# Delta-net layer: pair scales on VectorE, later transposes of keys and first values, head convolutions in two parts, gate sums beside the decays

## The chip, the core and the metric

The kernel runs on one core of a Trainium2 chip. The metric is the device time of one execution in microseconds. A core has five engines that run side by side and wait for each other by semaphores: TensorE (PE, matmuls; its weight loads, PEld, overlap them), VectorE (DVE), ScalarE (ACT), GpSimd (POOL), and SyncE (SP), which here issues most of the DMAs. Matmuls write to PSUM, of which this kernel keeps two pools of four banks, `ps` (tiles named `mm`) and `ps_acc` (tiles named `acc`); everything else lives in SBUF.

## What is computed

A trunk of two layers over 256 tokens of width 1024. Each layer is a SwiGLU block, a mixer and another SwiGLU block, with RMS norms around each. The mixer of the first layer is a short gated convolution, that of the second a gated delta-net with 8 key heads and 16 value heads of width 128. The change lies in the delta-net alone. Its core, cut down:

```python
qkv = silu(causal_depthwise_conv(x @ w_qkv, conv_w))         # width 4
q, k = l2norm(q), l2norm(k)                                   # repeated for two value heads each
beta = sigmoid(b); g = -exp(a_log) * softplus(a + dt_bias)    # per token and value head
g = cumsum(g) in a chunk
decay = exp(g_c - g_s) below the diagonal
a = strict_lower(beta * (k @ k.T) * decay)
t_inv = inverse(eye + a)
u, w = t_inv @ (beta * v), t_inv @ (beta * k * exp(g))
for each chunk:
    v_new = u - w @ state
    o = (q * exp(g)) @ state + lower(q @ k.T * decay) @ v_new
    state = state * exp(g_last) + (k * exp(g_last - g)).T @ v_new
return (o * rsqrt(mean(o * o) + eps) * norm_w * silu(z)) @ w_out
```

## The kernel before

The tokens are two tiles of 128 (`NT`), and a chunk here is one such tile. Every weight matrix streams from HBM in units of 128 x 1024 floats. `unit` (L108) loads one into `raw`, ScalarE rounds it to `whi` (L117), and VectorE takes the rest, `wlo = raw - whi` (L119); three matmuls then stand for one of full precision. Three `raw` buffers and eight of each half bound how far the stream runs ahead.

The layer's stream on TensorE is: the head (`head_slabs`, L218 to L222) with the gates' columns and the first seven key and query tiles, for both token tiles; nine key and query tiles in groups of 24 matmuls of 256 columns (`stat_group`, L275 to L277); three slabs of z (`act_group`, L218 to L222, 512 columns); four slabs of values (`v_group`, four `stat_group`s each); the last slab of z; the output projection (`out_proj`, L320 to L322).

Beside this stream run chains, Python generators under a `Ticker` (L89). A tick falls after every 12 matmuls of `stat_group` (two in a group) and after every 6 of `act_group` (eight in a slab of z, both token tiles together). `yield k` puts the rest of a chain k ticks further back in the text of the program. The text sets a priority only: the build works out when the operands of each instruction should be ready, orders every engine's queue by that and by the text, and what it puts out is fixed. An engine works through its queue in order, so an instruction whose operands come later than the build expected holds up all that follow. `tc.issue_after` adds an order by hand.

The chains that matter here:

- `gates` (L504) works out beta and the log decays g on POOL, ACT and DVE, and ends with two small matmuls (L531, L532) that sum g along a tile, and their exponentials `etail` and `eg`.
- `decays` (L536) multiplies a triangle with g (`gu`, mostly L545 on DVE), waits until a convolved head is there (`convs`), and then makes the eight decay tiles: a matmul (L553), an exponential (L555), a mask on POOL (L556). Two pairs' tiles are written in one tick, the others in the next; a tick later the silus of the waiting heads follow.
- `head_tail` (L888) transposes the head's last tile and convolves the seven head tiles. `conv` (L580) is one ACT operation (L581) and three DVE operations (L583). `kq_raw` calls it for a key or query tile and, when a head has both, passes the head on to silu (L570).
- `kq_chain` (L602) takes the heads in four pairs. Each head, `KQ_WAIT` ticks after its silu, is transposed (L615) and multiplied with itself (L618); ACT squares and sums the transposed tiles (L627). A tick after the second head, the sums get EPS (L631, POOL), keys are inverted (L633, DVE), `dd` = beta / |k|^2 (L636, POOL), and eight DVE operations (L642) write the scaled and decayed products, which frees their PSUM. ACT copies the diagonal blocks of 32 to `Ld` (L649). POOL also makes `nk` (a power, L651), `eq` and `wt`. After the last pair `invert` starts.
- `invert` (L664) inverts all 32 blocks' diagonals at once: a transpose (L666), 31 steps of two DVE operations (L674, L676), two transposes (L678, L680). `INV_WAIT` ticks later TensorE joins the blocks in two halves (L704 to L736), with the diagonals copied into `E` (L696) and `KQ` (L686) by POOL.
- `v_pair` (L745) convolves two value tiles, takes their silu, waits `V_WAIT` ticks, transposes them (L754) and scales them into `nv`. Its buffer `vc` is named `yb`, of which there are two.
- `scan` (L794) of a pair starts when its values and its inverse are there: solves (L768), products inside a chunk (L777), the state (L808, L817), and the same for the second tile; `z_chain` (L838) applies the norm and z, transposes (L848) and splits the result into the operands of the output projection (L851, L852).

Of the kernel before, what the change touches and what calls it, by code (L numbers as in the profile page):

```python
# [10 lines left out]
ALU = mybir.AluOpType  # L11
# [4 lines left out]
NT = 2  # L16
D = 1024
KD = D // P
# [3 lines left out]
NG = 4  # L22
B32 = 32
EPS = 1e-6
# [5 lines left out]
NSMALL = 22  # L30
NBIG = 8
NROW = 3
KQ_WAIT = 3
INV_WAIT = 37
V_WAIT = 4
SCAN_WAIT = 2
ORD = "00111222"
GORD = "00012222"
# [11 lines left out]
def trunk_kernel(ctx: ExitStack, tc: tile.TileContext, x, norm_g, w_gu, w_dn, sc_in, sc_cw, sc_out,  # L50
                 gdn_h0, gdn_h1, gdn_a0, gdn_a1, gdn_a2, gdn_v, gdn_z, gdn_cw, gdn_al, gdn_dt, gdn_nw, gdn_out, eye, upper, slower, out, stop=None):
    nc = tc.nc
    V, S, G, PE = nc.vector, nc.scalar, nc.gpsimd, nc.tensor
# [71 lines left out]
    def slab(shape, dtype, name):  # L125
        return hp.tile(shape, dtype, name=name, tag="slab")

    def big(shape, dtype, name):
        return bp.tile(shape, dtype, name=name, tag="big")
# [343 lines left out]
    def gdn_proj(xh, xl, mid):  # L473
# [22 lines left out]
        def bc(ap, n):  # L496
            return ap.unsqueeze(1).broadcast_to([P, n, ap.shape[-1]])

        def side_bank():
            return (ps if tail[0] else ps_acc).tile([P, 4, P], F32, name="mm" if tail[0] else "acc")  # L500
# [3 lines left out]
        def gates():  # L504
            def sm(name):
                return sp.tile([P, NT, NVH], F32, name=name, bufs=1)

            a, u, e, z, q = sm("ga"), sm("gb"), sm("gc"), sm("gd"), sm("ge")
            G.tensor_tensor(a, ba[:, :, NVH:], bc(dtb, NT), ALU.add)
            G.tensor_scalar(u, a, 0.0, -2.0, ALU.max, ALU.mult)  # L510
            G.tensor_tensor(e, a, u, ALU.add)
            first = S.activation(e, e, AF.Exp).ins
            with tc.issue_after(first):
                S.activation(al, al, AF.Exp)
            S.activation(beta, ba[:, :, 0:NVH], AF.Exp, scale=-1.0)

            V.tensor_scalar(z, e, 2.0, None, ALU.add)
            V.reciprocal(z, z)
            V.tensor_tensor(z, z, e, ALU.mult)
            V.tensor_tensor(u, z, z, ALU.mult)  # L520
            V.tensor_scalar(q, u, 1.0 / 19.0, None, ALU.mult)
            for k in (17, 15, 13, 11, 9, 7, 5, 3):
                V.scalar_tensor_tensor(q, q, 1.0 / k, u, ALU.add, ALU.mult)
            V.scalar_tensor_tensor(q, q, 1.0, z, ALU.add, ALU.mult)
            V.tensor_scalar(a, a, 0.0, None, ALU.max)
            V.scalar_tensor_tensor(q, q, 2.0, a, ALU.mult, ALU.add)
            V.scalar_tensor_tensor(g, q, -1.0, bc(al, NT), ALU.mult, ALU.mult)
            G.tensor_scalar(beta, beta, 1.0, None, ALU.add)
            V.reciprocal(beta, beta)
            pg = side_bank().rearrange("p a b -> p (a b)")[:, 0:2 * NVH].rearrange("p (t n) -> p t n", t=NT)  # L530
            PE.matmul(pg[:, 0, :], lhsT=tri_s, rhs=g[:, 0, :], start=True, stop=True)  # L531
            PE.matmul(pg[:, 1, :], lhsT=tri_u, rhs=g[:, 1, :], start=True, stop=True)  # L532
            S.activation(etail, pg[:, 0, :], AF.Exp)
            S.activation(eg, pg[:, 1, :], AF.Exp)

        def decays():  # L536
            gus = []
            for gi in range(NG):
                gu = big([P, NT, 4, P], F32, "gu")
                for t in range(NT):  # L540
                    if 2 * gi + t < GUACT:
                        for hv in range(4):
                            S.activation(gu[:, t, hv, :], tri_u, AF.Copy, scale=g[:, t, 4 * gi + hv:4 * gi + hv + 1])
                        continue
                    V.tensor_tensor(gu[:, t], bc(tri_u, 4),  # L545
                                    g[:, t, 4 * gi:4 * gi + 4].unsqueeze(2).broadcast_to([P, 4, P]), ALU.mult)
                gus.append(gu)
            while not convs:
                yield 1
            for gi in range(NG):  # L550
                for t in range(NT):
                    pd = side_bank()
                    PE.matmul(pd, lhsT=tri_s, rhs=gus[gi][:, t], start=True, stop=True)  # L553
                    d = slab([P, 4, P], F32, "dec")
                    last_exp[0] = S.activation(d, pd, AF.Exp).ins  # L555
                    G.affine_select(d, d, pattern=[[0, 4], [1, P]], compare_op=ALU.is_ge, fill=0.0, base=0,  # L556
                                    channel_multiplier=-1)
                    dec[t][gi] = d
                if gi % 2:
                    yield 1  # L560
            dec_done[0] = True
            while convs:
                kq_silu(*convs.pop(0))
# [12 lines left out]
        KQ = [[None] * NT for _ in range(NG)]  # L576
# [6 lines left out]
                V.scalar_tensor_tensor(dst[:, j:], src[:, 0:T - j], cw[:, ch, 3 - j:4 - j],  # L583
                                       dst[:, j:], ALU.mult, ALU.add)

        raws, kq_time = {}, [0] * KD

        def kq_raw(kh, c, src):
            if kh not in raws:
                raws[kh] = slab([P, 2, T], F32, "kq")  # L590
            conv(raws[kh][:, c, :], src, c * KD + kh)
            if c == 1:
                if dec_done[0]:
                    kq_silu(kh, raws[kh])
                else:
                    convs.append((kh, raws[kh]))

        def kq_silu(kh, t_):
            silu(t_, t_)
            kq[kh], kq_time[kh] = t_, tk.now  # L600

        def kq_chain():  # L602

            for gi in range(NG):
                ss = sp.tile([P, NT, 2, 2], F32, name="kss", bufs=2)
                k1 = slab([P, 2, 2, P], F32, "kq1")
                pkq = []
                for i in range(2):
                    kh = 2 * gi + i
                    while kq[kh] is None or tk.now < kq_time[kh] + KQ_WAIT:  # L610
                        yield 1
# [16 lines left out]
                    yield 1  # L628
                while dec[1][gi] is None:
                    yield 1  # L630
                G.tensor_scalar(ss, ss, EPS, None, ALU.add)  # L631
                rk = sp.tile([P, NT, 2], F32, name="rk", bufs=2)
                V.reciprocal(rk, ss[:, :, 0, :])  # L633
                dd = small(f"dsc{gi}", 8).rearrange("p (t n) -> p t n", t=NT)
                for t in range(NT):
                    G.tensor_tensor(dd[:, t, :].rearrange("p (k v) -> p k v", k=2),  # L636
                                    beta[:, t, 4 * gi:4 * gi + 4].rearrange("p (k v) -> p k v", k=2),
                                    rk[:, t, :].unsqueeze(2).broadcast_to([P, 2, 2]), ALU.mult)
                for t in range(NT):
# [5 lines left out]
                    for b in range(4):  # L645
                        r = slice(b * B32, (b + 1) * B32)
# [7 lines left out]
                w = small(f"wt{gi}", 4)  # L654
                G.tensor_tensor(w, etail[:, 4 * gi:4 * gi + 4], dd[:, 0, :], ALU.mult)
                Dsc[gi], nk[gi], eq[gi], wt[gi] = dd, n, q, w
                yield 1
            tk.start(invert())


# [3 lines left out]
        def invert():  # L664
# [14 lines left out]
            Yd = row("blk").rearrange("p (a b) -> p a b", a=B32)  # L679
            V.transpose(Yd.rearrange("p h i -> p i h"), X)  # L680
            T1 = row("blk").rearrange("p (a b) -> p a b", a=B32)
            for gi in range(NG):
                for t in range(NT):
                    for b in range(4):
                        r = slice(b * B32, (b + 1) * B32)
                        G.tensor_copy(KQ[gi][t][r, :, 0, r], Yd[r, 8 * gi + t:8 * gi + t + 7:2, :])  # L686
            yield INV_WAIT
            for half in range(2):
                hs = slice(16 * half, 16 * half + 16)
                gis = (2 * half, 2 * half + 1)  # L690
                E = {}
                for gi in gis:
                    E[gi] = slab([P, 8, 64], F32, "E64")
                    for b in range(2):
                        r = slice(b * B32, (b + 1) * B32)
                        G.tensor_copy(E[gi][r, :, r], Xd[r, 8 * gi:8 * gi + 8, :])  # L696
                    G.memset(E[gi][0:B32, :, B32:], 0.0)
                pt = side_bank().rearrange("p a (b c) -> p (a b) c", c=B32)
                for x in range(16):
                    ht = 16 * half + x  # L700
# [5 lines left out]
                for b in (1, 3):  # L706
                    r = slice(b * B32, (b + 1) * B32)
# [37 lines left out]
        def v_pair(gi, i, pt, tiles):  # L745
            vc = sp.tile([P, 2, T], F32, name="yb")
            for j in range(2):
                conv(vc[:, j, :], pt[:, j, :], 16 + 4 * gi + 2 * i + j)
            silu(vc, vc)
            yield V_WAIT  # L750
            tp = ps.tile([P, NT, 2, P], F32, name="mm")
            for t in range(NT):
                for j in range(2):
                    PE.transpose(tp[:, t, j, :], vc[:, j, t * P:(t + 1) * P], ident)  # L754
            for t in range(NT):
                S.activation(tiles[t][:, 2 * i:2 * i + 2, :], tp[:, t, :, :], AF.Copy,
                             scale=nk[gi][:, t, i:i + 1])
            if i == 1:
                nv[gi] = tiles
# [106 lines left out]
        order = [(kh, c) for kh in range(KD) for c in range(2)]  # L866
# [21 lines left out]
        def head_tail(late):  # L888
            yield 1
            late()  # L890
            for kh, c in order[0:7]:
                kq_raw(kh, c, craw[kh][:, c, :])

        tk.start(head_tail(head_slabs([load_slab(gdn_h0, GSPLIT, GORD), load_slab(gdn_h1, GSPLIT, GORD[4:])], xh, xl, evac_head, mid, 0)))
# [148 lines left out]
```

## Time and profile before

| | |
|---|---|
| median of 3 runs | 1130.77 us (1130.25 to 1133.5) |
| the profiled execution | 1131.77 us, of which the span of the profile is 1129.9 us |
| mean granted clock of TensorE | 0.994 of full speed |
| delta-net layer in the profile | head from 664 us, key tiles from 690 us, z and values to 880 us, output projection from 884 us |
| TensorE idle in the span, stretches over 0.12 us | 20.5 us, of which 14.4 us between 684 and 840 us |

In the views quoted below a row of the timeline holds the start and the time in us, engine, line, operation, destination and sources, shape and number, and in brackets how long the engine was idle before it and who ended that. A row of waits holds the waiter, the releaser, total us, times and the longest. A row of stretches holds the stretch, its length, the busy time of each engine with its instructions, the granted clock, the DMA share and GB/s. Rows of one line or tile give shortest, median and longest time in ns, and the first and last start.

### The profile page before, as it was taken

The numbers are of one execution on the slowest core, as the hardware profiler recorded it, in microseconds if no ns is written. First come the engines' busy times: TensorE is split into PE (matmuls) and PEld (weight loads), VectorE is DVE, ScalarE is ACT, GpSimd is POOL, SyncE is SP. The second block draws the span as 40 slices with busy tenths as digits, with TensorE's granted clock in tenths as the row PEclk, the third lists the DMA queues.
The fourth block names the chain that finished last, engine by engine and source line by source line (L and its number), as shares of the span: only waits on it lengthen the run. The fifth ranks groups of instructions, "written<-read, shape, count | busy, mean of one in ns | idle before, by whom it ended". The sixth has DMA issues, their size and how long they took to land.

```text
span 1129.9 us, 16843 instructions
## 1 busy us (share of the span) xinstructions
PE 1102.4 (98%) x6286; PEld 943.4 (83%) x6286; DVE 747.8 (66%) x1137; ACT 651.8 (58%) x1201; POOL 87.9 (8%) x167
## 2 busy tenths in 40 slices
PE   9999999999999999999999999889899999999997
PEld 6888887788788888788888877768899887888886
DVE  5776735687777673577765478768956557767543
ACT  6666635545566653556664458784587645666432
POOL 0000000000200000010000012110151212000000
PEclk9999999999999999999999999999899999999999
DMA  7755555666575555566555653327342355655552
GB/s 256 246 175 206 175 178 173 212 181 205 186 221 193 183 200 161 164 226 211 191 190 168 190 187 114 94 94 226 110 133 76 127 164 165 221 199 182 192 168 75
DMA packets 55955, 198.12 MB, mean 175 GB/s; under 512 B 6721, under 2 KB 7233, under 8 KB 55874
## 3 DMA queue, kind: packets, MB, share of 16 engines
q1 hardware_dynamic: 55728, 196.99, 53.9%
q8 instruction: 49, 0.80, 0.3%
q14 instruction: 32, 0.26, 0.1%
q10 hardware_dynamic: 146, 0.07, 0.0%
HBM read 195.99 MB, written 1.05 MB: 174 GB/s over the span
## 4 chain that ended last, share of the span: by engine, by line
PE 81%; DVE 6%; ACT 5%; issue 2%; POOL 2%; DMA 2%; DVEq 0%; POOLq 0%; ACTq 0%
PE mm L295 27%; PE mm L298 14%; PE acc L321 7%; PE acc L320 7%; PE acc L322 7%; PE mm L218 3%; PE mm L219 3%; PE mm L222 3%; DVE wlo L119 2%; ACT whi L117 1%; ACT blk L649 1%; PE mm L173 1%; DVE kq L583 1%; ACT junk L145 1%; PE mm L276 1%
## 5 line engine op out<-in xcount | busy, mean ns | idle before, releaser
L119 DVE TENSOR_TENSOR wlo<-raw,whi 128x1024 fp32r<-128x1024 f32 (+2 forms) x362 | 437.3, 1220 | 239.0 <-ACT whi L117 201.0
L117 ACT ACTIVATE whi<-raw 128x1024 fp32r<-128x1024 f32 (+2 forms) x362 | 375.8, 1051 | 221.7 <-PE acc L322 104.5
L295 PE MATMUL mm<-x,whi 128*128 128x512 f32 x1312 | 329.3, 393 | 0.0
L295 PEld LDWEIGHTS mm<-x,whi 128*128 128x128 f32 x1312 | 235.9, 189 | 42.3
L298 PEld LDWEIGHTS mm<-x,wlo 128*128 128x128 f32 x1312 | 179.0, 190 | 12.9
L298 PE MATMUL mm<-x,wlo 128*128 128x256 f32 x1312 | 182.9, 282 | 0.0
L320 PE MATMUL acc<-whi,hb 128*128 128x512 f32 x352 | 136.5, 388 | 0.0
L321 PE MATMUL acc<-wlo,hb 128*128 128x512 f32 x352 | 135.6, 385 | 0.3 <-DVE wlo L119 0.3
L322 PE MATMUL acc<-whi,hb 128*128 128x512 f32 x352 | 135.3, 385 | 0.0
L305 ACT ACTIVATE corr<-mm 128x256 f32<-128x256 f32 x164 | 61.1, 376 | 72.9 <-PE mm L298 71.9
L219 PE MATMUL mm<-wlo,x 128*128 128x512 f32 (+1 forms) x240 | 94.1, 393 | 1.8 <-DVE wlo L119 1.8
L218 PE MATMUL mm<-whi,x 128*128 128x512 f32 (+1 forms) x240 | 95.0, 396 | 0.4 <-ACT x L175 0.2
L222 PE MATMUL mm<-whi,x 128*128 128x512 f32 (+1 forms) x240 | 87.8, 389 | 0.0
L321 PEld LDWEIGHTS acc<-wlo,hb 128*128 128x128 f32 x352 | 66.2, 188 | 13.7 <-DVE wlo L119 0.8
L322 PEld LDWEIGHTS acc<-whi,hb 128*128 128x128 f32 x352 | 66.1, 188 | 13.3
L320 PEld LDWEIGHTS acc<-whi,hb 128*128 128x128 f32 x352 | 66.2, 188 | 13.1
L151 POOL TENSOR_SCALAR rstd<-ss 128x1 f32<-128x1 f32 x24 | 12.3, 510 | 787.9 <-ACT junk L145 787.9
L275 PE MATMUL mm<-x,whi 128*128 128x256 f32 x200 | 60.3, 302 | 2.0 <-DVE kq L583 2.0
L276 PE MATMUL mm<-x,whi 128*128 128x256 f32 x200 | 59.0, 296 | 0.0
L277 PE MATMUL mm<-x,wlo 128*128 128x256 f32 x200 | 58.6, 293 | 0.0
L219 PEld LDWEIGHTS mm<-wlo,x 128*128 128x128 f32 x240 | 45.4, 189 | 12.1 <-DVE wlo L119 3.6
L218 PEld LDWEIGHTS mm<-whi,x 128*128 128x128 f32 x240 | 45.3, 189 | 10.4 <-ACT x L175 2.0
(213 smaller groups left out, 1238.0 us busy)
## 6 DMA issues: line engine op xcount, KB each, us to landing
raw<-in_w_gu SPq DMA_DIRECT2D x176, 512.0 KB, 4.2
raw<-in_w_dn SPq DMA_DIRECT2D x88, 512.0 KB, 3.6
raw<-in_sc_in SPq DMA_DIRECT2D x24, 512.0 KB, 4.1
raw<-in_gdn_z SPq DMA_DIRECT2D x16, 512.0 KB, 3.9
raw<-in_gdn_v SPq DMA_DIRECT2D x16, 512.0 KB, 4.3
raw<-in_gdn_out SPq DMA_DIRECT2D x16, 512.0 KB, 3.9
gamma<-in_norm_g SPq DMA_DIRECT2D x11, 512.0 KB, 5.4
raw<-in_gdn_a SPq DMA_DIRECT2D x9, 512.0 KB, 4.5
```

Of the source, the lines that this page charges most:

```text
L117: S.activation(hi[:, r], raw[:, r], AF.Copy)
L119: newest[0] = V.tensor_tensor(lo[:, r], raw[:, r], hi[:, r], ALU.subtract).ins
L218: PE.matmul(pt, lhsT=xh[:, t, k, :], rhs=hi, start=(k == 0), stop=False)
L219: PE.matmul(pt, lhsT=xh[:, t, k, :], rhs=lo, start=False, stop=False)
L222: PE.matmul(pt, lhsT=xl[:, t, j, :], rhs=part(j)[0], start=False, stop=(j == KD - 1))
L276: PE.matmul(ptile, lhsT=hi, rhs=l2, start=False, stop=False)
L295: PE.matmul(flat, lhsT=part(k, 0), rhs=xx[:, k].rearrange("p h t q -> p (h t q)"), start=(k == 0), stop=False)
L298: PE.matmul(flat[:, T:], lhsT=part(k, 1), rhs=xx[:, k, 0].rearrange("p t q -> p (t q)"), start=False, stop=(k == KD - 1))
L305: S.activation(c, pt[:, 1, :], AF.Copy)
L320: PE.matmul(o, lhsT=yh(c, t), rhs=hi[:, r], start=(c == 0), stop=False)
L321: PE.matmul(o, lhsT=yh(c, t), rhs=lo[:, r], start=False, stop=False)
L322: i = PE.matmul(o, lhsT=yl(c, t), rhs=hi[:, r], start=False, stop=(c == n - 1)).ins
```

## The change

Six edits in the delta-net layer.

1. The EPS and the scales `dd` of a pair are computed on VectorE instead of GpSimd.
2. A head's transposes come 5 ticks after its silu instead of 3 (`KQ_WAIT`), and 3 ticks lie between a pair's products and the next pair instead of 1 (`PAIR_WAIT`, a new name).
3. The transposes of the values come 9, 6, 4 and 4 ticks after the silu for the four pairs, instead of 4 for all.
4. Four of the seven head tiles are convolved first, the other three `CONV_WAIT` = 3 ticks later. Since a head's two tiles can now come in either order, `kq_raw` counts them in `parts`.
5. The two matmuls that sum the gates, with their exponentials (`gate_sums`), are written in `decays`, ahead of its first decay matmul, instead of at the end of `gates`.
6. In `invert` the copies of the diagonals into `KQ` are written in each half after the copies into `E`, instead of all at once ahead of the wait.

```diff
-KQ_WAIT = 3
+KQ_WAIT = 5
+PAIR_WAIT = 3
 INV_WAIT = 37
-V_WAIT = 4
+V_WAIT = (9, 6, 4, 4)
+CONV_WAIT = 3
@@
             G.tensor_scalar(beta, beta, 1.0, None, ALU.add)
             V.reciprocal(beta, beta)
+
+        def gate_sums():
             pg = side_bank().rearrange("p a b -> p (a b)")[:, 0:2 * NVH].rearrange("p (t n) -> p t n", t=NT)
             PE.matmul(pg[:, 0, :], lhsT=tri_s, rhs=g[:, 0, :], start=True, stop=True)
             PE.matmul(pg[:, 1, :], lhsT=tri_u, rhs=g[:, 1, :], start=True, stop=True)
@@
             while not convs:
                 yield 1
+            gate_sums()
             for gi in range(NG):
@@
-        raws, kq_time = {}, [0] * KD
+        raws, kq_time, parts = {}, [0] * KD, [0] * KD
@@
             conv(raws[kh][:, c, :], src, c * KD + kh)
-            if c == 1:
+            parts[kh] += 1
+            if parts[kh] == 2:
                 if dec_done[0]:
@@
-                G.tensor_scalar(ss, ss, EPS, None, ALU.add)
+                V.tensor_scalar(ss, ss, EPS, None, ALU.add)
                 rk = sp.tile([P, NT, 2], F32, name="rk", bufs=2)
                 V.reciprocal(rk, ss[:, :, 0, :])
                 dd = small(f"dsc{gi}", 8).rearrange("p (t n) -> p t n", t=NT)
                 for t in range(NT):
-                    G.tensor_tensor(dd[:, t, :].rearrange("p (k v) -> p k v", k=2),
+                    V.tensor_tensor(dd[:, t, :].rearrange("p (k v) -> p k v", k=2),
@@
                 Dsc[gi], nk[gi], eq[gi], wt[gi] = dd, n, q, w
-                yield 1
+                yield PAIR_WAIT
             tk.start(invert())
@@
-            for gi in range(NG):
-                for t in range(NT):
-                    for b in range(4):
-                        r = slice(b * B32, (b + 1) * B32)
-                        G.tensor_copy(KQ[gi][t][r, :, 0, r], Yd[r, 8 * gi + t:8 * gi + t + 7:2, :])
             yield INV_WAIT
             for half in range(2):
@@
                     G.memset(E[gi][0:B32, :, B32:], 0.0)
+                for gi in gis:
+                    for t in range(NT):
+                        for b in range(4):
+                            r = slice(b * B32, (b + 1) * B32)
+                            G.tensor_copy(KQ[gi][t][r, :, 0, r], Yd[r, 8 * gi + t:8 * gi + t + 7:2, :])
@@
-            yield V_WAIT
+            yield V_WAIT[gi]
@@
-            for kh, c in order[0:7]:
+            for i, (kh, c) in enumerate(order[0:7]):
+                if i == 4:
+                    yield CONV_WAIT
                 kq_raw(kh, c, craw[kh][:, c, :])
```

## The prediction

> **What bounds the kernel now.** I read the page first: TensorE is busy nearly all the time, so only its idle stretches, and stretches at a lower clock, can be won.
>
> ```profile
> span 1129.9 us, 16843 instructions
> ...
> PE 1102.4 (98%) x6286; PEld 943.4 (83%) x6286; DVE 747.8 (66%) x1137; ACT 651.8 (58%) x1201; POOL 87.9 (8%) x167
> ```
>
> Second, TensorE's waits over the two halves of the delta-net layer, 684 to 764 us and 764 to 900 us (waiter, releaser, total us, times, longest):
>
> ```profile
> PE acc L615 <- ACT kq L570: 3.6, 2, 3.1
> PE mm L275 <- DVE kq L583: 2.0, 1, 2.0
> PE acc L618 <- DVE KQ L642: 1.7, 1, 1.7
> PE mm L219 <- DVE wlo L119: 1.3, 1, 1.3
> PE acc L531 <- DVE glog L527: 0.7, 1, 0.7
> PE acc L615 <- ACT junk L627: 0.7, 2, 0.4
> ...
> PE mm L754 <- ACT yb L570: 3.8, 1, 3.8
> PE acc L715 <- ACT blk L708: 0.4, 1, 0.4
> ```
>
> With the 0.2 us of L704 below, that is 10.0 + 4.4 = 14.4 us, the most that waits can give back. Third, the timeline of PE for where the large ones lie (idle time in brackets):
>
> ```profile
> 709.90 0.39 PE L275 MATMUL mm<-x,whi 128*128 128x256 f32 x1 [1.98 <-DVE kq L583]
> ...
> 749.21 0.66 PE L615 MATMUL acc<-ident,kq 128*128 128x128 f32 x4 [3.06 <-ACT kq L570]
> ...
> 796.96 1.11 PE L754 MATMUL mm<-ident,yb 128*128 128x128 f32 x4 [3.75 <-ACT yb L570]
> ...
> 815.41 0.78 PE L704 MATMUL acc<-blk,KQ 32*32 32x32 f32 x37 [0.17 <-DVE blk L678]
> ```
>
> Fourth, busy time by stretch: PE, PEld, DVE, ACT, POOL, then granted clock and DMA. The last six are cut at the clock's own steps of 3.41 us:
>
> ```profile
> 716.00:760.00 44.00, 38.02 (x235) 33.56 (x235) 30.45 (x64) 39.34 (x119) 9.78 (x27) 1.00 0.30 89
> 760.00:816.00 56.00, 50.77 (x360) 46.78 (x360) 50.92 (x103) 29.34 (x41) 0.53 (x2) 0.94 0.58 175
> 840.00:900.00 60.00, 60.00 (x382) 54.28 (x383) 37.23 (x93) 43.02 (x122) 12.03 (x21) 1.00 0.33 106
> 706.77:710.18 3.41, 1.43 (x9) 0.98 (x8) 3.41 (x9) 1.33 (x4) 0.00 (x0) 1.00 0.00 0
> 710.18:713.59 3.41, 3.41 (x18) 3.41 (x18) 3.20 (x5) 1.92 (x10) 0.00 (x0) 0.50 0.41 125
> 744.31:747.72 3.41, 1.84 (x9) 1.19 (x7) 3.41 (x8) 3.34 (x11) 0.00 (x0) 1.00 0.00 0
> 792.10:795.51 3.41, 1.10 (x10) 0.90 (x8) 3.38 (x11) 1.82 (x3) 0.00 (x0) 1.00 0.12 47
> 795.51:798.92 3.41, 1.96 (x9) 1.97 (x10) 3.41 (x9) 3.19 (x6) 0.00 (x0) 0.50 0.15 20
> 798.92:802.34 3.42, 3.42 (x18) 3.42 (x17) 3.42 (x10) 1.56 (x3) 0.00 (x0) 0.50 0.55 147
> ```
>
> A step with PE busy 1.43 or 1.10 us is followed by one at half clock; with 1.84 (the 3.06 us wait lies across its end) it is not. So two waits cost more than themselves: the one at 710 by 3.41/2 = 1.7 us, the one at 797 by (1.96 + 3.42)/2 = 2.7 us. Waits and clock together are 18.8 us. Beside PE there is little slack where it waits: ACT is busy 39.3 of 44 us in 716 to 760, DVE 50.9 of 56 us in 760 to 816.
>
> The Trainium skill, "TensorE: Matmul & The Clock Gate", Part 1, says that the half clock comes after an idle window of about 3.4 us, windows running free of the kernel. Steps of 3.41 us agree; but here 1.98 us of idling was enough, and 3.06 us was not. By that rule neither 1.7 nor 2.7 us would go with the waits.
>
> **Head convolutions in two parts.**
>
> ```profile
> 694.66 0.48 DVE L583 SCALAR_TENSOR_TENSOR kq<-craw,gcw,kq 128x253 f32<-128x253 f32 x1
> 695.05 4.29 DVE L545 TENSOR_TENSOR gu<-tri_u,glog 128x512 f32<-128x512 f32 x7
> 699.27 8.62 DVE L583 SCALAR_TENSOR_TENSOR kq<-craw,gcw,kq 128x253 f32<-128x253 f32 x14
> ...
> 709.37 0.47 DVE L583 SCALAR_TENSOR_TENSOR kq<-mm,gcw,kq 128x253 f32<-128x253 f32 x1
> ```
>
> PE at 709.90 waits for the third operation of the first convolution from PSUM, which DVE reaches after 21 operations on craw. The change puts 9 of these behind it. Of the 12 left, 5 are done by then (the row at 694.66 is the fifth); 7 x 8.62/14 = 4.3 us and three of 0.47 end it near 705, ahead of 707.92, where PE began to wait. All 3.7 us can go; the 9 operations (some 4 us) then stand between DVE and the weight splits of the next slab, so I take 3.2 (0 to 3.7).
>
> **Gate sums with decays.**
>
> ```profile
> 694.79 0.39 PE L531 MATMUL acc<-glog,tri_s 128*128 128x16 f32 x2 [0.73 <-DVE glog L527]
> ```
>
> The sums are written ahead of the last head matmuls, yet ran amid those of the key slabs: the build places an instruction where it expects its operands. Written a tick later they still wait for glog, 0.7 us. I take 0.2 (0 to 0.7).
>
> **Pair scales on VectorE.**
>
> ```profile
> 729.83 0.24 POOL L631 TENSOR_SCALAR kss<-kss 128x8 f32<-128x8 f32 x1 [7.30 <-ACT junk L627]
> 730.16 1.05 POOL L651 TENSOR_TENSOR nk<-kss,phalf 128x4 f32<-128x4 f32 x1
> ...
> 731.61 0.35 POOL L636 TENSOR_TENSOR dsc<-beta,rk 128x4 f32<-128x4 f32 x2
> ...
> 730.11 0.18 DVE L633 RECIPROCAL rk<-kss 128x4 f32<-128x4 f32 x1 [2.68 <-POOL kss L631]
> 730.20 1.23 DVE L119 TENSOR_TENSOR wlo<-raw,whi 128x1024 fp32r<-128x1024 f32 x1
> 731.84 2.05 DVE L642 SCALAR_TENSOR_TENSOR KQ<-acc,dsc,dec 128x256 f32<-128x256 f32 x5 [0.41 <-POOL dsc L636]
> ```
>
> From the sums to the products is 731.84 - 729.83 = 2.0 us, half of it the power on POOL standing before the scales. On DVE it is four operations like the reciprocal, 0.7 us, or 2 us again if a weight split of 1.23 us is placed between them: about 1 us a pair is won. The three moved operations cost 12 x 0.18 = 2.2 us of DVE, hidden in 44 - 30.5 us of idling; uncovered they cost that. What waited was L618, for PSUM that the products still held: at most 1.0 of its 1.7 us.
>
> **Later transposes, and what moves with them.** A tick is 12 matmuls of 256 columns, 1.4 us:
>
> ```profile
> 715.36 0.28 PE L276 MATMUL mm<-x,whi 128*128 128x256 f32 x1
> ...
> 717.99 0.28 PE L277 MATMUL mm<-x,wlo 128*128 128x256 f32 x1
> ```
>
> (22 apart, 0.12 us each; a z tick, 6 of 512 columns, is alike.) With n the tick of the head convolutions, the silus of heads 0 to 3 are at n+3. Before, the four pairs are scaled at n+8, 11, 14 and 20 (the last waits for head 7, convolved at n+16) and the inverse starts at n+22. After, 5 ticks from silu to transpose and 3 between pairs give n+10, 15, 20, 25 and n+29. So each L615 has 2 to 8 ticks more of stream in front: the waits of L615 and L618, 6.0 us, could all go. But ACT has only 4.7 us idle in this stretch, and much of it is waiting for the same chain. I take half, 3.0 (0 to 6.0). The wait of 1.3 us for wlo stays (0): DVE's transpose L666 is queued ahead of it.
>
> **Later first values.** The 3.75 us before L754, with 2.7 us of clock, fall away if PE has 9 ticks of other matmuls (6 for the second pair, 4 as before for the others). But yb has two buffers: the second pair's first convolution, due at tick 12 of the value slabs, gets its buffer only from the transposes at tick 13, so ACT's L581 waits some 1.4 us, with roundings L117 behind it. And the matmuls need weight splits and convolutions from DVE, which has 5.1 us idle in 56. I take 4.0 of 6.4 (0 to 6.4).
>
> **The inverse.** Its result is read 37 ticks after its start, as before, so 7 ticks later: PE gets 7 x 1.4 = 10 us more to do ahead of L704, which now waits only 0.2 us for the inverse. DVE gets the load of those ticks too. The inverse's start on its timeline:
>
> ```profile
> 760.08 1.25 DVE L666 STREAM_TRANSPOSE blk<-blk 128x1024 f32<-128x1024 f32 x1 [2.02 <-ACT blk L649]
> ```
>
> A value slab (8 ticks) is 4 splits and 12 operations of a convolution, 4 x 1.23 + 12 x 0.47 = 10.6 us; 7 ticks are 9 us, against 5.1 us of idling. If L666 is no earlier, the inverse ends some 4 us later, and 10 - 4 = 6 us is all that can be won up to L704, where the terms above make 10.4. If the scales bring L666 forward by 4 us there is no loss. Half way: -2.2 (0 to -8).
>
> **The diagonal copies**, written after the inverse's E copies instead of ahead of them:
>
> ```profile
> L686 POOL COPY KQ<-blk x32: 286/289/1191, 818.8 to 831.1; 32x128 f32<-32x128 f32 x32
> ```
>
> The second half's E comes 16 x 0.29 = 4.6 us earlier, its copies later; the solves that read them run from 840 on, where PE is never idle: 0. Uncovered, it is 4.6 us.
>
> **The tail.** The first scans too come 7 ticks later, against a fixed end:
>
> ```profile
> 866.88 1.04 PE L848 MATMUL mm<-ident,zs 128*128 128x128 f32 x8
> ...
> 884.28 0.48 PE L320 MATMUL acc<-whi,hb 128*128 128x512 f32 x1
> ```
>
> The output projection's first operand was transposed 884.3 - 866.9 = 17 us before use; 7 ticks with the scans' own matmuls between them take most of it, and three scans now hold the PSUM banks that the projection takes over. ACT's 17 us of idling in 840 to 900 cover the rest: -1.0 (0 to -5).
>
> **Sum.** 3.2 + 0.2 + 3.0 + 4.0 - 2.2 - 1.0 = 7.0 us. The profiled execution took 1131.8 us (span 1129.9 and 1.9 around it), 1.0 above the median of 1130.8: so 1124.8 in a profile, and a median of **1123.8 us**.
>
> **Rivals.** About 0.3%, 3.4 us, is what a measurement of this kernel can tell from no change.
> - *Slower: the inverse is read too early.* Place: L704. If DVE falls behind by its whole 9 us of added load and the 5 us that were idle stay idle, L678 ends 14 us later than 815; PE has 10 us of work for it and waits 4 us, over half of a clock step, so 1.7 us more. All gains ahead of L704 are swallowed by that wait: 1131 + 4 + 1.7 = 1136 us. It decides once the inverse is more than 10 us late. For it: DVE at 91%. Against: the scales are won just ahead of L666. Chance 0.10.
> - *The tail waits.* Three scans share the four banks and ACT just ahead of the projection at 884; a wait of 4 us and a clock step instead of my 1.0 give 1123.8 + 4.7 = 1128.5. For: the order is fixed at the end. Against: ACT is 72% busy there. Chance 0.20.
> - *It does not do what it says.* As with the sums, instructions go where the build expects operands, not where they are written; the key waits then stay and half of the 4.0 with them, while the inverse is not later either: 1123.8 + 3.0 + 2.0 - 2.2 = 1126.6. For: L531. Against: L615 waits because it was expected too early, which more ticks cure. Chance 0.10.
> - *The waits go, the half clock stays.* If the steps at half clock do not come from these waits, their share in my terms, 1.5 and 1.6 us, is not won: 1126.9. The rows above speak against it. Chance 0.05. The rule of the Trainium skill's page above leads to this case.
> - *All of it goes, and DVE keeps up*: inverse and tail cost nothing, keys give 5.0, values 5.5: 1123.8 - 3.2 - 2.0 - 1.5 = 1117. Chance 0.18.
>
> **Numbers.** Forecast 0.37 (1120 to 1127 by itself). Range 1116 to 1131: it takes in all but the slower rival (0.10) and the edge of the last (0.06). Faster by over 0.3%, below 1127.4: the forecast 0.37, all gone 0.18, half clock 0.05, most of the third and a little of the second, 0.69 in all. Slower, above 1134.2: 0.10. Within: 0.21.
>
> **What would show it.** Right: no wait of L275 at the fourth key group and clock 1.00 around 710 (conv split); L642 within 1.2 us of the last square (scales); L615 waits under 1 us (transposes); no half clock near 795 (values). Wrong: L704 waiting for L678 or L680 by several us, L320's first waiting for ACT, DVE or PSUM, new waits of PE for wlo in 710 to 800, or a step at half clock after any of them.

## The result and the profile after

The change makes the kernel slower: 1136.98 us (median of 4 runs, 1136.91 to 1138.41) against 1130.55 us for the kernel before in the same session, ratio 1.0055, 95% interval [1.004, 1.007]. The profiled execution took 1137.03 us, of which the span is 1135.3 us. The forecast was 1123.8 us, range 1116 to 1131. Ratios and intervals here and below leave out runs more than 1.5% above the fastest of the same kernel: three of the twelve of one kernel, and one of the kernel before. Line numbers after: L704 is L710, L729 is L735, L754 is L760, L686 is L703, L696 is L697, L275 is L277, L219 is L221, L321 is L323, L531 is L535; in the kernels of the first experiment's edit L710, L735 and L760 are one higher.

The page after (busy time), and TensorE's waits from 684 to 920 us (waiter, releaser, total us, times, longest):

```profile
span 1135.3 us, 16852 instructions
...
PE 1106.0 (97%) x6286; PEld 946.9 (83%) x6286; DVE 748.0 (66%) x1149; ACT 651.9 (57%) x1201; POOL 84.3 (7%) x155
```

```profile
PE acc L735 <- POOL E L698: 7.6, 1, 7.6
PE mm L760 <- ACT yb L575: 3.2, 1, 3.2
PE mm L277 <- DVE kq L588: 2.6, 2, 2.0
PE mm L277 <- DVE yb L588: 1.0, 1, 1.0
PE acc L624 <- ACT junk L633: 1.0, 1, 1.0
PE acc L535 <- DVE glog L529: 0.7, 1, 0.7
```

The keys' waits (L615, L618 before; L621, L624 now) are nearly gone. A new one of 7.6 us stands at the 64x64 block products L735, for POOL, an engine that is busy 7% of the time. It is no lack of speed but an order. GpSimd's timeline, before and then after:

```profile
815.42 1.73 POOL L696 COPY E<-blk 32x256 f32<-32x256 f32 x4 [60.14 <-DVE blk L678]
...
818.82 12.55 POOL L686 COPY KQ<-blk 32x128 f32<-32x128 f32 x32
```

```profile
815.53 14.96 POOL L703 COPY KQ<-blk 32x128 f32<-32x128 f32 x32 [54.89 <-DVE blk L686]
830.54 0.82 POOL L697 COPY E<-blk 32x256 f32<-32x256 f32 x2
831.41 0.30 POOL L698 MEMSET E<- 32x256 f32 x1
```

Before, the first half's copies into E went first, from 815.42, and the 32 copies into KQ after them. (The text of the kernel before had it the other way round, the 32 copies ahead of E: the order on GpSimd was the build's.) After, all 32 go first, 15 us of them, and the first E is whole at 831.71. TensorE stood there until 831.76. What follows is the second part of the loss. TensorE's rows, and the stretches cut at the clock's steps (PE, PEld, DVE, ACT, POOL busy, then the granted clock):

```profile
831.76 1.97 PE L735 MATMUL acc<-E,KQ 64*64 64x64 f32 x16 [7.63 <-POOL E L698]
...
838.71 3.67 PE L742 MATMUL acc<-KQ,E 64*64 64x64 f32 x32
842.31 1.92 PE L710 MATMUL acc<-blk,KQ 32*32 32x32 f32 x64
```

```profile
822.79:826.20 3.41, 1.34 (x12) 1.13 (x10) 2.51 (x4) 3.27 (x10) 3.08 (x9) 1.00 0.59 165
826.20:829.61 3.41, 0.00 (x0) 0.00 (x0) 0.00 (x0) 0.52 (x2) 2.89 (x11) 0.96 0.34 135
829.61:833.02 3.41, 1.26 (x12) 1.26 (x13) 0.00 (x0) 0.00 (x0) 2.95 (x10) 0.50 0.00 0
833.02:836.44 3.42, 3.42 (x26) 3.08 (x25) 0.00 (x0) 1.22 (x2) 2.12 (x6) 0.50 0.00 0
836.44:839.85 3.41, 3.41 (x23) 3.07 (x22) 1.45 (x3) 1.07 (x2) 0.00 (x0) 0.50 0.00 0
839.85:843.26 3.41, 3.41 (x60) 3.29 (x60) 0.93 (x1) 2.24 (x5) 0.00 (x0) 0.50 0.02 5
843.26:846.68 3.42, 3.42 (x50) 3.36 (x46) 0.30 (x1) 2.36 (x5) 0.00 (x0) 0.55 0.53 153
```

The cuts lie 0.3 us late, as the 0.96 and the 0.55 show: the clock halves at 829.3 and stays there for five steps, 17.1 us, to 846.4, though from 833 on TensorE is busy without a gap. Before, it was at full speed from 802 us to the end of the layer.

### The profile page after: what moved, and what is told of

Its sections match the earlier page's. It is cut to its first block, busy times and chain, and to the rows that moved or that the text cites. A ratio compares the mean times of both kernels' runs of the same rounds, so it can differ in the third digit from the quotient of the medians.

```text
span 1135.3 us, 16852 instructions
## 1 busy us (share of the span) xinstructions
PE 1106.0 (97%) x6286; PEld 946.9 (83%) x6286; DVE 748.0 (66%) x1149; ACT 651.9 (57%) x1201; POOL 84.3 (7%) x155
## 4 chain that ended last, share of the span: by engine, by line
PE 81%; DVE 8%; ACT 4%; POOL 3%; issue 3%; DMA 1%; POOLq 0%; DVEq 0%; ACTq 0%; SPq 0%
PE mm L297 27%; PE mm L300 14%; PE acc L323 7%; PE acc L324 7%; PE acc L322 7%; PE mm L220 3%; PE mm L221 3%; PE mm L224 3%; DVE wlo L121 2%; ACT whi L119 1%; POOL KQ L703 1%; PE mm L175 1%; ACT blk L655 1%; ACT junk L147 1%; DVE yb L588 1%
## 5 line engine op out<-in xcount | busy, mean ns | idle before, releaser
L323 PE MATMUL acc<-wlo,hb 128*128 128x512 f32 x352 | 135.6, 385 | 0.4 <-DVE wlo L121 0.4
L221 PE MATMUL mm<-wlo,x 128*128 128x512 f32 (+1 forms) x240 | 93.7, 391 | 0.5 <-DVE wlo L121 0.5
L323 PEld LDWEIGHTS acc<-wlo,hb 128*128 128x128 f32 x352 | 66.2, 188 | 13.6 <-DVE wlo L121 0.7
L277 PE MATMUL mm<-x,whi 128*128 128x256 f32 x200 | 60.5, 302 | 3.6 <-DVE kq L588 2.6
L221 PEld LDWEIGHTS mm<-wlo,x 128*128 128x128 f32 x240 | 45.4, 189 | 10.6 <-DVE wlo L121 2.5
```

The lines of the kernel that those rows point to most:

```text
L221: PE.matmul(pt, lhsT=xh[:, t, k, :], rhs=lo, start=False, stop=False)
L277: PE.matmul(ptile, lhsT=hi, rhs=h2, start=(k == 0), stop=False)
L323: PE.matmul(o, lhsT=yh(c, t), rhs=lo[:, r], start=False, stop=False)
```

## The experiments

The theory after the result (A): only E's late place in GpSimd's queue makes the change slow, and the keys' waits of 5 and 3, which put the inverse and what follows it seven ticks further back in the text, brought it about. The rival (B): the copies into KQ, which the change moved (its last edit), or the load on the engines, make it slow. All ratios are to the kernel before, run on the same chip; where two kernels are compared, the price is the difference of their ratios times 1131 us.

### E early

The E tiles are taken, and their zero quarter written, ahead of the inverse's wait. The copies into E and KQ stay where the change has them.

```diff
+            E = {}
+            for gi in range(NG):
+                E[gi] = slab([P, 8, 64], F32, "E64")
+                G.memset(E[gi][0:B32, :, B32:], 0.0)
             yield INV_WAIT
...
-                E = {}
...
-                    E[gi] = slab([P, 8, 64], F32, "E64")
...
-                    G.memset(E[gi][0:B32, :, B32:], 0.0)
```

> The changed kernel, with the four E tiles taken and their lower blocks cleared ahead of the INV_WAIT instead of behind it, so that E has its slab buffers early; all copies stay where the change has them. Theory A (E gets its buffer late, so GpSimd makes all 32 diagonal copies first and TensorE waits 7.6 us for E and then runs some 15 us at half clock): E is copied first, the wait of 7.6 us and the half clock after it go, 1120 to 1126 us. Theory B (the later inverse overloads VectorE or the tail, and E only happens to be the last of what is late): another wait at the joining of the blocks or at the output projection takes its place, 1132 us or more.

Measured: 1124.24 us, ratio 0.9936 [0.9924, 0.9948]. GpSimd's timeline of this kernel:

```profile
815.09 3.56 POOL L699 COPY E<-blk 32x256 f32<-32x256 f32 x6 [52.18 <-DVE blk L684]
818.71 7.97 POOL L704 COPY KQ<-blk 32x128 f32<-32x128 f32 x16
```

E is first again, and TensorE no longer waits for it. All that the change was to win is there; the lateness of E had cost 13.5 us ((1.0055 - 0.9936) x 1131).

### The inverse read seven ticks sooner

```diff
-INV_WAIT = 37
+INV_WAIT = 30
```

> The changed kernel with INV_WAIT 30 instead of 37, so that the joining of the blocks stands where it stood before the change, 59 ticks after the head convolutions. Theory A: the buffers are free there, E is copied first, no long wait for E: 1120 to 1127 us. Theory B (the inverse itself comes too late because the keys do): TensorE now waits for the inverse's transposes on VectorE instead, by up to 7 us, 1130 us or more.

Measured: 1124.99 us, ratio 0.9943 [0.9929, 0.9957]. E's copies run from 815.57, ahead of those into KQ; TensorE's wait at L735 is 0.4 us, for ScalarE's part of E (L725). The seven ticks are the cause: with them the same kernel takes 12.7 us more ((1.0055 - 0.9943) x 1131).

### The kernel before, with the inverse read seven ticks later

```diff
-INV_WAIT = 37
+INV_WAIT = 44
```

> The kernel before with INV_WAIT 44 instead of 37 and nothing of the change: the joining of the blocks is written 7 ticks later. Theory A: E gets its buffers late here too, GpSimd makes the 32 diagonal copies first, TensorE waits 5 us or more for E and runs at half clock after it: 1137 to 1146 us. Rival: the place alone does no harm, only the edits together do: 1128 to 1133 us.

Measured: 1137.37 us, ratio 1.0051 [1.0039, 1.0063]: the seven ticks alone, without any other part of the change, make the kernel before as slow as the change does. TensorE's row:

```profile
835.87 1.38 PE L729 MATMUL acc<-E,KQ 64*64 64x64 f32 x15 [2.39 <-POOL E L697]
```

The idle time is only 2.4 us here, since this kernel also keeps its older waits and TensorE comes later; two steps at half clock follow, from 836.6 us.

### The last edit undone

The copies into KQ go back ahead of the inverse's wait, the rest is the change.

```diff
+            for gi in range(NG):
+                for t in range(NT):
+                    for b in range(4):
+                        ...
+                        G.tensor_copy(KQ[gi][t][r, :, 0, r], ...)
             yield INV_WAIT
...
-                for gi in gis:
-                    for t in range(NT):
-                        ...
-                            G.tensor_copy(KQ[gi][t][r, :, 0, r], ...)
```

> The changed kernel with the sixth edit undone: the diagonal copies are written ahead of the INV_WAIT, all at once, as before. Theory A: E still gets its buffers late and comes behind the 32 copies: 1135 to 1139 us, as the changed kernel. Theory C (the moved copies are what pushed E back): E is first again and the time is 1120 to 1126 us.

Measured: 1138.94 us, ratio 1.0068 [1.0056, 1.008], with 7.1 us at L735. Rival B falls: where the copies are written makes no difference clear of noise, and E early, which leaves the load on the engines as it was, had already won the time back.

### What each part gives, once E is in time

First a control, E early in the kernel before (the diff of the first experiment, applied there).

> The kernel before with E early and nothing else: a control for the kernels built on E early. The theory: what E early wins over the changed kernel (1124.2 against 1137) is only the lateness that the change brought about, and the kernel before, whose E was written in time, gains nothing from it: 1130 to 1132, ratio 0.998 to 1.002, with no wait at the first block products for E. The rival: E early is a gain by itself, and the change's own parts gave little: then 1125 to 1128, ratio 0.994 to 0.997.

Measured: 1131.16 us, ratio 1.0001 [0.9992, 1.001]. E early is worth nothing by itself, so the 7 us are the change's own. Then one part at a time was undone, on top of E early.

The split of the head convolutions:

```diff
-                if i == 4:
-                    yield CONV_WAIT
```

> The kernel with E early (1124.2, ratio to before 0.9936), with the seven convolutions of the head issued in one part again. The prediction priced the split at 3.2 us; if that price is right, this gives 1127.4, ratio about 0.9965, and the fourth key group's first matmul (L277) waits longer than the 2.0 us it still waits with the split. The theory after the first runs: the split is worth nothing (0 to 0.5 us), since VectorE's work in front of that convolution is as long in either case and the wait has only moved with the stream; then 1124 to 1125, ratio 0.993 to 0.995, with the wait at L277 near 704 us between 1.5 and 2.5.

Measured: 1126.36 us, 0.9954 [0.994, 0.9968]. The split is worth about 2 us, between both expectations, and the intervals just overlap. The wait at L277 is 2.2 us against 2.0 with the split; what is new are 1.4 us at L221 for the weight split and 1.4 us more at L277 for the values' convolution (2.4 against 1.0).

The waits of the values:

```diff
-V_WAIT = (9, 6, 4, 4)
+V_WAIT = (4, 4, 4, 4)
```

> The kernel with E early, with all waits of the values back at 4. The prediction priced the later transposes at 4.0 us: then 1128.2, ratio about 0.997, with TensorE's wait at L761 back at pair 0's first half near 790 (3 to 4 us) and two half-clock steps behind it. The theory after the first runs: the wait has only gone from pair 0 to pair 1 (3.3 us there with E early), and what was won is at most the clock of one step, 1 to 1.7 us: then 1125 to 1126, ratio 0.994 to 0.9955. If both halves wait, pair 0's as before and pair 1's as now, it is the prediction's price.

Measured: 1129.95 us, 0.9971 [0.9954, 0.9988], so 4 us, the prediction's price. Two rows of TensorE's waits:

```profile
PE mm L761 <- ACT yb L575: 4.2, 1, 4.2
...
PE acc L736 <- ACT E L726: 1.1, 1, 1.1
```

Pair 0's transposes wait again, and then the second wait, of 1.1 us among the block products, is followed by three steps at half clock, from 829.1 to 839.4 us. This does not happen in every run: four of the twelve took 1122.5 to 1124.8 us, at a mean clock of 0.995 to 0.997, no more than E early; the other eight took 1129.7 to 1131.5 us at 0.987 to 0.992. So in these runs the price is that of the half clock, and a median of few runs depends on how often it comes.

The waits of the keys:

```diff
-KQ_WAIT = 5
-PAIR_WAIT = 3
+KQ_WAIT = 3
+PAIR_WAIT = 1
```

> The kernel with E early, with the keys' waits back at 3 and 1 (the scales stay on VectorE). If the waits give the bulk, as the waits at L621 and L624 say (7.3 us before with the recurrence's load, 1.5 with E early), this gives 1129 to 1131, ratio about 0.999. By the prediction's price of 3.0 it gives 1127.2, ratio 0.997. If the scales on VectorE have shortened the keys' chain by themselves, so that the waits are hardly needed, it gives 1124 to 1125.5, ratio 0.994 to 0.995, with L621 and L624 waiting under 2.5 together.

Measured: 1127.93 us, 0.9965 [0.9952, 0.9978], so about 3.3 us. L621 and L624 wait 3.3 us together (0.8, 2.1 and 0.4), with E early 1.0.

The pair scales:

```diff
-                V.tensor_scalar(ss, ss, EPS, None, ALU.add)
+                G.tensor_scalar(ss, ss, EPS, None, ALU.add)
...
-                    V.tensor_tensor(dd[:, t, :].rearrange(...), ...)
+                    G.tensor_tensor(dd[:, t, :].rearrange(...), ...)
```

> The kernel with E early, with the pair scales' three operations back on GpSimd. If the longer waits of the keys alone cover the chain, this changes nothing: 1124 to 1125, ratio 0.993 to 0.995. If the scales' way over GpSimd is part of the keys' path even with the longer waits (about 1 us for each of four pairs, as the prediction had it), L621 and L624 wait 2 to 4 us more and it gives 1126 to 1128, ratio 0.996 to 0.9975.

Measured: 1128.63 us, 0.9974 [0.9965, 0.9983], so about 4.3 us. But it is not L621 and L624 that wait (0.8 us); new waits stand elsewhere, 2.0 us at L221 for the weight split, 3.9 us at L277 for the values' convolution (the profile is of one of the longer runs, 1130.41 us). The expectation had the size nearly right and the place wrong.

The gate sums, back in `gates` (the fifth edit undone; the expectation names another place and number):

```diff
-        def gate_sums():
...
-            gate_sums()
```

> The kernel with E early, with the gate sums back in the decay block (edit 3 undone). The prediction had 0.2 us for it (0 to 0.7). The wait at L535 is there with the edit and without it (0.73 before, 0.95 with E early), so the same: 1124 to 1125, ratio 0.993 to 0.995. If the sums' place also decides when the convolutions get VectorE, 1126 or more.

Measured: 1126.17 us, 0.9954 [0.994, 0.9967], so about 2 us, though the sums wait about as long either way (0.7 us at what is L533 there, 0.9 with E early). Again the waits move: 3.9 us at L277 for the values' convolution, where there was 1.0.

Undone singly, the five cost 2.0, 4.0, 3.3, 4.3 and 2.0 us, 15.6 in all, where all five together gain 7.2 (0.0064 x 1131). They do not add. By the intervals each price carries about 2 us either way, so the two of 2.0 are at the edge of what can be told, and the excess of the sum, 8.4 us, carries some 6 (estimates). In three of the five (convolutions, scales, sums) new waits stand in the stretch of the values, at L277 and L221: an edit elsewhere in the text gave VectorE another order there. How much of each price that is was not measured.

### Pair 1's transposes later too

On E early, to win the 3.3 us that L761 still waits.

```diff
-V_WAIT = (9, 6, 4, 4)
+V_WAIT = (9, 9, 4, 4)
```

> The kernel with E early and waits of the values of 9, 9, 4, 4: pair 1's transposes three steps later too. Left to win there: 3.3 us at L761 near 803 and one half-clock step (up to 1.7 us). If nothing later waits: 1119 to 1122, ratio 0.990 to 0.992. If the wait only goes on to the next pair, as it went from pair 0 to pair 1: 1123.5 to 1125, ratio 0.993 to 0.995.

Measured: 1127.15 us as the median of all twelve runs, from 1121.61 to 1144.09; ratio 0.9951 [0.9931, 0.9971] without the three above 1141. The wait at L761 is gone, and one of 1.7 us has come at the 32x32 products. TensorE's row, and the stretches at the clock's steps:

```profile
816.87 1.83 PE L711 MATMUL acc<-blk,KQ 32*32 32x32 f32 x64 [1.75 <-DVE blk L684]
```

```profile
813.99:817.40 3.41, 1.66 (x32) 1.33 (x32) 3.41 (x5) 1.45 (x2) 0.46 (x2) 0.95 0.77 255
817.40:820.82 3.42, 3.42 (x60) 3.36 (x55) 3.42 (x5) 1.88 (x3) 3.22 (x5) 0.50 0.11 40
...
834.47:837.88 3.41, 3.41 (x28) 3.19 (x27) 1.62 (x5) 0.00 (x0) 0.02 (x1) 0.55 0.00 0
```

1.75 us of idling are followed by 20.5 us at half clock. This is the slower rival's place (the inverse read too early), reached by another way. The stretch need not come in each run: the mean granted clock of the twelve goes from 0.999 (1122.64 us) to 0.973 (1144.09 us), and only one run, of 1131.91 us, was profiled.

### What in the seven ticks makes E late

Still open was the link from the seven ticks to E's place. E takes its buffers from the same pool ("slab") as the values' `nv`, and in the text its first write moved from ahead of the third group's `nv` to behind it. So the third group's wait alone was changed, in the kernel with the whole change and nothing of E early.

```diff
-V_WAIT = (9, 6, 4, 4)
+V_WAIT = (9, 6, 8, 4)
```

> The changed kernel with one number changed: the third wait of the values 8 in place of 4; the inverse, E and the copies are as the change has them. The theory in its sharper form: the build gives the slab buffers out in the order in which the text first writes their tiles. The change's seven ticks put E's first write behind that of the third group's nv, so E waits for a buffer until nv's first writer is due, with buffers free all along. Four ticks more for that nv put E ahead again. Then GpSimd makes E's copies first from about 815 us, TensorE waits under 1 us for E, and the time is 1122 to 1126, ratio 0.992 to 0.996, as with E early. If a shortage of buffers, or the lateness of E's own text, is what counts, a later nv changes nothing for E: 1135 to 1139, with 7 us at L735.

```diff
-V_WAIT = (9, 6, 4, 4)
+V_WAIT = (9, 6, 5, 4)
```

> The same with 5 in place of 4: one tick. By the same theory this is enough for the first half's two E tiles (GpSimd makes them ahead of the 32 diagonal copies) and not for the second half's, which come behind all 32, from about 830 us. TensorE then has the first half's block products on time and waits for E before the second half's, some 1 to 4 us, with a stretch of half clock behind it: 1127 to 1134, ratio 0.997 to 1.003. If E's lateness goes by the seven ticks and not by the neighbour, one tick of another chain changes nothing: 1135 to 1139.

Measured: with 8, 1128.8 us, 0.9984 [0.9971, 0.9998]; with 5, **1123.84 us, 0.9937 [0.9923, 0.9951]**. One tick of another chain takes 13.3 us off the changed kernel and makes it as fast as E early (0.9937 and 0.9936). GpSimd and TensorE with 5:

```profile
813.95 1.72 POOL L697 COPY E<-blk 32x256 f32<-32x256 f32 x4 [53.06 <-DVE blk L684]
815.71 0.30 POOL L698 MEMSET E<- 32x256 f32 x1
816.07 14.59 POOL L703 COPY KQ<-blk 32x128 f32<-32x128 f32 x32
830.72 1.88 POOL L697 COPY E<-blk 32x256 f32<-32x256 f32 x2
```

```profile
824.38 1.11 PE L735 MATMUL acc<-E,KQ 64*64 64x64 f32 x16
...
828.31 2.08 PE L742 MATMUL acc<-KQ,E 64*64 64x64 f32 x32
830.32 1.20 PE L710 MATMUL acc<-blk,KQ 32*32 32x32 f32 x64
```

As the theory said, one tick brings the first half's E ahead of the 32 copies and leaves the second half's behind them, and four ticks bring both ahead. Two parts of the expectations missed. With 5, the second half's late E (830.72) costs nothing: TensorE has other work until then. With 8, E is in time, but the second half of the third group's values is transposed at 846.2 instead of 834.7 us, and a new wait stands later, in the recurrence of the last group:

```profile
884.06 1.10 PE L814 MATMUL mm<-yw,ktok 128*128 128x256 f32 x4 [2.74 <-DVE yw L807]
```

This pair of kernels also splits the loss. With 4 and with 5 TensorE does nearly the same until 817 us (L710 starts at 816.80 and 816.96); the second half's L710 starts at 842.31 and 830.32, 12.0 us apart, the ends of the spans 13.2 us apart. 7.6 us are the wait. The rest, 5.6 us, is the half clock: 3.67 us for the 32 products of L742 against 2.08 is a factor of 1.76, and the 14.9 us that TensorE was busy in the five slow steps, times (1 - 1/1.76), make 6.4 us, an estimate.

That the neighbour's `nv` decides is shown. That it does so because buffers are given out in the order of first writes is the reading that foretold both orders on GpSimd; a shortage that a later `nv` happens to relieve would look alike in these two runs. Against a shortage speaks the order that the build puts out. In it E's first write comes directly behind that of the `nv` ahead of it in the text: the second group's before the change and with 8, the third group's with the change, and with 5 the second group's for the first half and the third's for the second half. And in the changed kernel six of the pool's 22 buffers stand free at that place. No run was made with more buffers, for a 23rd does not fit.

## Why the prediction failed

**The diagonal copies: 0, since "the second half's E comes 16 x 0.29 = 4.6 us earlier, its copies later". This is the step that failed, together with the seven ticks of the inverse.** It took GpSimd's queue to follow the text. It did not: all 32 copies went ahead of all E. Nor had it before the change, where the text has the 32 copies first: the row of L686 that the prediction quotes begins at 818.8, behind E's copies from 815.42. The edit itself is worth nothing, as forecast (undone: 1138.94). But no step asked from which pool E gets its buffers and who stands ahead of it. The prediction had the rule it needed, "the build places an instruction where it expects its operands", and used it for the gate sums and a rival, not here.

**The inverse: -2.2, for VectorE's load of 9 us against 5.1 us of idling.** This is the term that was wrong in the sum. The seven ticks were right, but they cost 12.7 us in the changed kernel and 5.8 in the kernel before, and by GpSimd's order, not by VectorE's load. The inverse was not late at all:

```profile
765.65 1.25 DVE L672 STREAM_TRANSPOSE blk<-blk 128x1024 f32<-128x1024 f32 x1 [0.51 <-ACT blk L655]
...
813.37 2.09 DVE L686 STREAM_TRANSPOSE blk<-blk 128x1024 f32<-128x1024 f32 x1
```

It started 5.6 us later than before (760.08) and its last transpose was over at 815.5, before at 817.2 (815.25 + 1.97); L710 at 816.80 waits for nothing. The slower rival gave nearly the right time, 1136 us, at the wrong place: L704 for the inverse, not L729 for E. So it was not this rival that came true. Of the signs that the prediction listed for being wrong, none was a wait for E.

**The rest of the sum.** Without the lateness of E the change gives 1123.84 or 1124.24 us, and the forecast was 1123.8. That is in part luck, since the terms were less good than their sum:

- *Head convolutions, 3.2:* the wait did not go. It stayed 2.0 us and came 3 us earlier:

```profile
706.90 0.39 PE L277 MATMUL mm<-x,whi 128*128 128x256 f32 x1 [2.00 <-DVE kq L588]
...
699.41 5.47 DVE L588 SCALAR_TENSOR_TENSOR kq<-craw,gcw,kq 128x253 f32<-128x253 f32 x7
...
706.38 0.47 DVE L588 SCALAR_TENSOR_TENSOR kq<-mm,gcw,kq 128x253 f32<-128x253 f32 x1
```

  VectorE was done near 707, not 705. The seven operations took 0.85 us each, as long as GpSimd's masks ran beside them (698.4 to 705.4 us); the 0.62 of the prediction was a mean over such operations and those of 0.47 behind the masks. And two operations on craw ran between the three on PSUM. TensorE came at 704.90, not 707.92: the first keys' matmuls, 1.5 us in front of this group before, now come behind it by the keys' own edit, and of the key slabs' matmuls 10 instead of 22 ran between the decay matmuls and the wait. What the split gives, some 2 us, it gives elsewhere. The sign named for it, clock 1.00 around 710, was there without its cause: the wait fell otherwise on the clock's steps.
- *Keys, 3.0 of 6.0:* L615, L618 and the wlo wait made 7.3 us before; 1.0 us at L624 is left of them, with 0.6 us at L277; the wlo wait, which the prediction let stay, went too. Undoing the longer waits costs 3.3 us. The forecast was too low for the waits, right for the time.
- *Pair scales, 1 us a pair:* the step itself was right; from the last square to the first product there are now 1.2 us:

```profile
730.78 0.19 ACT L633 ACTIVATION_READ_ACCUMULATOR junk<-acc 128x1 f32 x1
...
731.01 0.17 DVE L637 TENSOR_SCALAR kss<-kss 128x8 f32<-128x8 f32 x1 [2.36 <-ACT junk L633]
...
731.98 3.22 DVE L648 SCALAR_TENSOR_TENSOR KQ<-acc,dsc,dec 128x256 f32<-128x256 f32 x8
```

- *Values, 4.0:* undone, 4.0 us, though by two kinds of runs, as above. But of the wait nothing was won: 3.75 us at pair 0 before, 3.2 at pair 1's first half and 1.0 for a convolution now. What was won is clock, one slow step (805.4 to 808.8) in place of two, and the place of the later waits.
- *Gate sums, 0.2:* L535 waits as before, as forecast; undone they cost about 2 us, at the edge of noise, with a longer wait in the values' stretch, which was not foreseen.
- *Tail, -1.0:* no wait of note arose there; L323 waits 0.4 us, 0.3 before.

## What to carry over

When an edit moves work back in the text, list the tiles that it allocates, the pool of each and its neighbours in that pool, and ask which of them are now first written earlier; an idle engine can then take its instructions in another order, and the lateness shows at the far end. Look for the fault with one number at a time: here a single tick of an unrelated chain took back 13 us. And price an edit by undoing it within the finished kernel, but do not add such prices, and look at the single runs before trusting a median.

## What the runs showed of the hardware

The half clock is worst where the matmuls are small. After 1.1, 1.75, 2.4 and 7.6 us of idling among the block products (32 to 64 rows and columns), the clock stayed at half for 3, 6, 2 and 5 steps of 3.41 us, with TensorE busy throughout in most of them; after 2.0 us at L277 and 3.2 us at L760, among matmuls of 128x128 with 256 columns, for one step or none (two, in the kernel before, behind the 3.75 us at L754). Block products at full clock do not by themselves lower it: with the third wait at 5 the stretch from 819 to 840 us ran at 1.00. The Trainium skill, "TensorE: Matmul & The Clock Gate", Part 1, says that the full clock returns after one busy window of about 3.4 us; that agrees behind L760 and not here, where three busy steps in the rows of the result were each followed by another slow one.

How busy a step must be to keep the full clock can be read when the steps are cut where the clock itself changes. Between 684 and 900 us of all the profiles, every step at full clock with TensorE busy for 1.50 us or less was followed by half clock. Those with 1.72 us or more were followed by full clock, but for one: the step with the 1.1 us wait among the block products, busy for 2.6 us. Between the two lie three steps: 1.61 us (half clock followed), 1.65 (full) and 1.66 (half). So the wait of 2.0 us at L277 cost a step in the profile with the third wait at 5, where 1.40 us of the step were busy, and none in the changed kernel, where 1.9 us were: the same wait, cut otherwise by the steps. That small products count for less in what sets the clock would fit the one exception and the long slow stretches; no run tested it alone.
